# The gates of a recurrence: the weights' low part on half of the array's rows, both heads in one call

## The chip, the cores and the metric

One NeuronCore of a Trainium2 chip runs the whole layer. The metric is the device time of one execution in microseconds (us); lower is better.

## What is computed

One layer of a generator over latent tokens: 512 latent and 256 context tokens, 2048 channels, float32. The part that the change touches are the gates of the recurrence (RG-LRU): 16 heads of 64 channels, two directions, and for each a 64 by 64 matrix for the gate r and one for the gate i.

```
hl = rmsnorm(x) * (1 + sc) + sh                  # adaLN, modulation from silu(c) @ w_ada
b, c, u, g, v, q = split(hl @ w_in)              # and the same for the context
ya = b * conv(c * u) * silu(g)
xb = conv(v) + bias                              # 1024 channels, latent and context
r = sigmoid(blockdiag(xb, wa) + ba)              # per direction, 16 heads of 64
i = sigmoid(blockdiag(xb, wx) + bx)
log_a = -8 * r * softplus(-lam);  a = exp(log_a)
h = scan(a, sqrt(1 - exp(2 log_a)) * i * xb)     # forward and backward
out = rmsnorm(x + gt * (concat(ya, (h_f + h_b) * silu(q)) @ w_out))
```

## The kernel before

Products in float32 accuracy are made of float32r matmuls (one pass each): an operand is split into a high part and a low part, the rest, and high x high, high x low and low x high are added up in PSUM. `mm3` (lines 81 to 85) issues these three matmuls for the projections. `split_piece` (line 331) splits a piece of 1024 columns of weights: ScalarE copies the high part (line 73), VectorE subtracts (line 74).

The program has three stages on TensorE. First the adaLN products (`ada`, line 216; its matmuls carry line 223 in the profile) alternate with the first seven tiles of the projection: `ada` multiplies plain float32 operands on tiles of 128 rows by 32 columns of the array, four of them side by side, each writing 32 partitions of PSUM. Then the loop over the remaining pieces of the projection (line 616), one step for each piece of eight 128-row blocks; last the output projection. The order of the work is written out by hand: the tables `bg` and `mid` list for each step which functions run at its end or after its fourth block of matmuls. For each group m of 128 channels (two heads) and from a step b on: `l_prep` at b, one call of `l_gate` in the middle of each of the steps b+2 to b+5, `l_ix` at b+3 and b+5, `l_exp` at b+5, and then the scan. There are eight groups, so 32 calls.

`l_prep` (line 444) makes the operands. The weights `lwh` and `lwl` are the high and low parts of a tile of 128 partitions, in which the 64 rows of a head's matrices stand twice, on partitions 0 to 63 and again on 64 to 127; its 512 columns are two directions by two heads by 128 (64 for r, 64 for i). The moving operand `xs` is a tile for each head: for head 0 the high part of the head's 64 channels on partitions 0 to 63 and the low part on 64 to 127, for head 1 the other way round. A product over all 128 partitions thus gives the weights times high plus low.

`l_gate` (line 459) handles one direction and one head for all 768 columns (512 latent, 256 context): two matmuls with the high weights (512 and 256 columns, lines 468 and 469), two with the low weights (lines 470 and 471), all over 128 partitions, into a PSUM tile `plru` of two banks that exists once (bufs=1). Then two sigmoids of 64x768 on ScalarE (lines 474 and 475) write `lr` and `li`; the next call's first matmul has to wait until both have read `plru`. ScalarE runs in order, so the copies of `split_piece` stand behind these sigmoids.

Of the kernel before, what the change touches and what calls it, by code (L numbers as in the profile page):

```python
# [9 lines left out]
AF = mybir.ActivationFunctionType  # L10
# [6 lines left out]
T = 512  # L17
TC = 256
TA = T + TC
# [30 lines left out]
def tile_hybrid_layer(ctx, tc, xt, ct, xn, wada, wgt, bgt, wa_, wbc, wout, lruw, par, ident, fg, out):  # L50
    nc = tc.nc
# [39 lines left out]
    def pc(name, i=0, n=1):  # L91
        o, w = POFF[name]
        return pt[:, o + i:o + i + n]
# [157 lines left out]
    for j in range(4):  # L251
        nc.tensor.matmul(acc[5][:, 2 * j:2 * j + 2], ssum[:, 128 * j:128 * j + 128], cmean[:, 0:2],
                         start=True, stop=True, skip_group_check=True)
# [188 lines left out]
    lru = {}  # L442
# [13 lines left out]
            xs.append(t)  # L456
        lru.update(w=(hi, lo), xs=xs)

    def l_gate(m, d, h):
        hi, lo = lru["w"]  # L460
        x = lru["xs"][h]
        if h == 0:
            lru["r", d] = lp[0].tile([128, TA], F32, name="lr", bufs=3)
            lru["i", d] = lp[0].tile([128, TA], F32, name="li", bufs=3)
        ps = pa.tile([128, 2, 512], F32, name="plru", bufs=1)
        pf = ps.rearrange("p a b -> p (a b)")
        s = slice(128 * (2 * d + h), 128 * (2 * d + h) + 128)
        nc.tensor.matmul(pf[:, 0:T], hi[:, s], x[:, 0:T], start=True, stop=False)  # L468
        nc.tensor.matmul(pf[:, T:TA], hi[:, s], x[:, T:TA], start=True, stop=False)
        nc.tensor.matmul(pf[:, 0:T], lo[:, s], x[:, 0:T], start=False, stop=True)  # L470
        nc.tensor.matmul(pf[:, T:TA], lo[:, s], x[:, T:TA], start=False, stop=True)  # L471
        b = pc("gb", 4 * m + 2 * d + h)
        o = slice(64 * h, 64 * h + 64)
        nc.scalar.activation(lru["r", d][o], pf[0:64, :TA], AF.Sigmoid, bias=b[0:64])  # L474
        nc.scalar.activation(lru["i", d][o], pf[64:128, :TA], AF.Sigmoid, bias=b[64:128])  # L475

    def l_ix(m, d):
        nc.gpsimd.tensor_tensor(lru["i", d], lru["i", d], xb[m], op=ALU.mult)  # L478
# [71 lines left out]
    for m in range(NM):  # L550
        b = S_C0 + 7 * m
        if m:
            at(b, l_sqrt, m - 1)
        at(b, l_prep, m)
        if m:
            at(b + 1, l_scan, m - 1)
        for i in range(4):
            at(b + 2 + i, l_gate, m, i // 2, i % 2, q=mid)
        at(b + 3, l_ix, m, 0)
        at(b + 5, l_ix, m, 1)  # L560
        at(b + 5, l_exp, m)
        if m + 1 < NM:
            at(b + 5, lw_load, m + 1)
        at(b + 6, l_mul, m)
# [6 lines left out]
    for j in range(4):  # L571
        b = S_C0 + 1 + 2 * j + 4 * (j // 2)
# [43 lines left out]
    for s in range(N_BC):  # L616
        ti, half = divmod(s, 2)
        n, m = BC_TILES[ti]
# [12 lines left out]
        hi, lo = wsp.pop(s)  # L631
# [4 lines left out]
        for k in range(8):  # L636
# [4 lines left out]
            w = slice(128 * k, 128 * k + 128)  # L641
            mm3(accs[ti][0], hi[:, w], lo[:, w], hlat[kk], kk == 0, kk == KT - 1)
        if n == "v":
            for k in range(8):
                kk = 8 * half + k
                w = slice(128 * k, 128 * k + 128)
# [68 lines left out]
    for q in range(N_D):  # L715
        s = N_BC + q
        c, kp = divmod(q, 8)
# [14 lines left out]
        hi, lo = wsp.pop(s)  # L732
# [98 lines left out]
```

## Time and profile before

| | us |
|---|---|
| median of 3 runs (811.78 to 813.51) | 812.3 |
| the profiled execution | 810.92 |
| its span | 809.1 |
| TensorE matmuls busy | 786.8 (97%) |
| VectorE busy | 480.4 (59%) |
| ScalarE busy | 366.8 (45%) |
| GpSimd busy | 89.7 (11%) |

The span runs from the first to the last instruction of the program; busy time is the time in which at least one instruction of the engine ran. PE is TensorE's matmul, PEld its loading of the stationary operand, which the profile lists as an engine of its own; DVE is VectorE, ACT is ScalarE, POOL is GpSimd. Matmuls are pipelined: one lasts longer than the distance to the start of the next.

### The profile page before, as it was taken

To read this page: it belongs to the slowest core of one execution; us is meant where nothing else is said; L and a number is where in the kernel's file an instruction comes from. 1 tells how busy PE (TensorE), PEld (TensorE's weight loads), DVE (VectorE), ACT (ScalarE), POOL (GpSimd) and SP (SyncE) were. 2 spreads that over 40 slices of the span, in tenths; PEclk is the share of its full clock that TensorE was granted. 3 is DMA by queue.
4 is the path that set the end of the run, shared out by engine and by line. 5 is a ranking of instruction groups with operands and counts; after the bars stand their busy time and mean duration, and the time that the engine had idled before them with its cause. 6 is when DMAs were issued, how large, how long until landed. Compare 5 with 4: busy or idle time off the path is not lost.

```text
span 809.1 us, 13525 instructions
## 1 busy us (share of the span) xinstructions
PE 786.8 (97%) x5712; PEld 678.2 (84%) x5712; DVE 480.4 (59%) x643; ACT 366.8 (45%) x458; POOL 89.7 (11%) x64
## 2 busy tenths in 40 slices
PE   7899899999999999999999999999999999999995
PEld 2688687889999998888888888888888888888884
DVE  3644444888688677283829474666476834253665
ACT  4312224451111125768576857575858532222234
POOL 0000002500000000212020202020212002020200
PEclk9999999999999999999999999999999999999999
DMA  9999996225655664232323232323231753323205
GB/s 352 417 417 415 347 353 218 98 79 187 227 184 180 226 222 153 79 116 80 120 76 122 96 121 79 118 78 118 79 124 58 309 185 92 116 81 128 79 0 208
DMA packets 36494, 136.31 MB, mean 168 GB/s; under 512 B 4049, under 2 KB 6353, under 8 KB 31697
## 3 DMA queue, kind: packets, MB, share of 16 engines
q1 hardware_dynamic: 36434, 135.45, 47.0%
q8 instruction: 45, 0.74, 0.4%
q14 instruction: 15, 0.12, 0.0%
HBM read 131.24 MB, written 4.19 MB: 167 GB/s over the span
## 4 chain that ended last, share of the span: by engine, by line
PE 95%; DMA 1%; DVE 1%; issue 1%; ACT 1%; SPq 0%; ACTq 0%
PE bacc L83 22%; PE bacc L84 22%; PE bacc L85 21%; PE bacc L741 6%; PE bacc L742 6%; PE bacc L743 6%; PE bacc L223 4%; DMA xhi<-in_xt 1%; PE plru L470 1%; PE plru L468 1%; PE plru L85 1%; PE plru L742 1%; PE plru L741 1%; PE plru L84 1%; PE plru L83 1%; PE plru L743 1%
## 5 line engine op out<-in xcount | busy, mean ns | idle before, releaser
L84 PE MATMUL bacc<-xhi,wlo 128*128 128x512 f32 x736 | 280.5, 381 | 2.4 <-issue 1.8
L83 PE MATMUL bacc<-xhi,whi 128*128 128x512 f32 x736 | 281.0, 382 | 0.8 <-ACT xhi L202 0.4
L85 PE MATMUL bacc<-hlo,whi 128*128 128x512 f32 x736 | 279.2, 379 | 2.6 <-issue 2.5
L74 DVE TENSOR_TENSOR wlo<-raw,whi 128x1024 fp32r<-128x1024 f32 (+1 forms) x129 | 157.6, 1225 | 198.9 <-ACT whi L73 197.6
L73 ACT CAST whi<-raw 128x1024 fp32r<-128x1024 f32 (+1 forms) x129 | 132.7, 1031 | 211.6 <-PE bacc L85 116.3
L84 PEld LDWEIGHTS bacc<-xhi,wlo 128*128 128x128 f32 x736 | 139.1, 189 | 25.2 <-DVE wlo L74 5.1
L85 PEld LDWEIGHTS bacc<-hlo,whi 128*128 128x128 f32 x736 | 139.1, 189 | 22.7 <-issue 2.9
L83 PEld LDWEIGHTS bacc<-xhi,whi 128*128 128x128 f32 x736 | 139.1, 189 | 22.5 <-ACT whi L73 0.7
L741 PE MATMUL bacc<-whi,yhi 128*128 128x512 f32 x224 | 85.1, 380 | 0.5 <-DVE dg L671 0.5
L742 PE MATMUL bacc<-wlo,yhi 128*128 128x512 f32 x224 | 84.9, 379 | 0.0
L743 PE MATMUL bacc<-whi,ylo 128*128 128x512 f32 x224 | 84.9, 379 | 0.0
L478 POOL TENSOR_TENSOR li<-li,xb 128x768 f32<-128x768 f32 x16 | 30.8, 1925 | 365.3 <-ACT li L475 365.3
L474 ACT ACTIVATE lr<-plru,pt 64x768 f32<-64x768 f32 x32 | 28.7, 895 | 53.2 <-PE plru L471 53.0
L267 ACT ACTIVATE xhi<-xhi,sh 128x512 fp32r<-128x512 f32 x15 | 10.8, 723 | 85.9 <-DVE xhi L266 85.9
L741 PEld LDWEIGHTS bacc<-whi,yhi 128*128 128x128 f32 x224 | 42.3, 189 | 7.1 <-DVE dg L671 1.1
L743 PEld LDWEIGHTS bacc<-whi,ylo 128*128 128x128 f32 x224 | 42.3, 189 | 6.0
L742 PEld LDWEIGHTS bacc<-wlo,yhi 128*128 128x128 f32 x224 | 42.3, 189 | 6.0
L518 DVE SCALAR_TENSOR_TENSOR gacc<-raw,cs,gacc 128x1024 f32<-128x1024 f32 x32 | 39.6, 1278 | 0.0
L223 PEld LDWEIGHTS bacc<-rada,cs 128*32 128x32 f32 x2048 | 29.6, 110 | 6.8 <-issue 6.8
L84 PE MATMUL bacc<-xchi,wlo 128*128 128x256 f32 x128 | 35.2, 275 | 0.0
L85 PE MATMUL bacc<-hclo,whi 128*128 128x256 f32 x128 | 35.2, 275 | 0.0
L83 PE MATMUL bacc<-xchi,whi 128*128 128x256 f32 x128 | 35.2, 275 | 0.0
(168 smaller groups left out, 876.3 us busy)
## 6 DMA issues: line engine op xcount, KB each, us to landing
raw<-in_wbc SPq DMA_DIRECT2D x82, 512.0 KB, 3.5
rada<-in_wada SPq DMA_DIRECT2D x32, 1024.0 KB, 10.4
raw<-in_wgt SPq DMA_DIRECT2D x32, 512.0 KB, 4.7
raw<-in_wout SPq DMA_DIRECT2D x32, 512.0 KB, 3.5
raw<-in_wa_ SPq DMA_DIRECT2D x16, 448.0 KB, 11.2
xhi<-in_xt SPq DMA_DIRECT2D x16, 256.0 KB, 4.5
xr<-in_xn SPq DMA_DIRECT2D x4, 1024.0 KB, 7.7
xchi<-in_ct SPq DMA_DIRECT2D x16, 128.0 KB, 4.4
```

The costliest lines, as they stand in the source:

```text
L73: nc.scalar.copy(hi[:, :n], raw[:, :n])
L74: nc.vector.tensor_tensor(lo[:, :n], raw[:, :n], hi[:, :n].bitcast(F32), op=ALU.subtract)
L83: nc.tensor.matmul(acc, wh, hh, start=first, stop=False)
L84: nc.tensor.matmul(acc, wl, hh, start=False, stop=False)
L85: nc.tensor.matmul(acc, wh, hl, start=False, stop=last)
L223: nc.tensor.matmul(o[32 * q:32 * q + 32], cs[:, 8 * p + j, :], r[:, j, q, :], start=p + j == 0, stop=p + j == 8, skip_group_check=True)
L474: nc.scalar.activation(lru["r", d][o], pf[0:64, :TA], AF.Sigmoid, bias=b[0:64])
L478: nc.gpsimd.tensor_tensor(lru["i", d], lru["i", d], xb[m], op=ALU.mult)
L518: nc.vector.scalar_tensor_tensor(gacc[:, s], gtq.pop(i), cs[:, k, 0:1], gacc[:, s], op0=ALU.mult, op1=ALU.add)
L741: nc.tensor.matmul(accs[t], yh[:, ts], wh, start=kk == 0, stop=False)
L742: nc.tensor.matmul(accs[t], yh[:, ts], wl, start=False, stop=False)
L743: nc.tensor.matmul(accs[t], yl[:, ts], wh, start=False, stop=kk == KT - 1)
```

## The change

One call of `l_gate` now handles one direction, both heads and half of the columns (384). The high products come first, one for each head, over all 128 partitions, each into a bank of its own. The low products follow, one for each head, over the 64 partitions only on which that head's high part stands (0 to 63 for head 0, 64 to 127 for head 1); the product of the two low parts is left out. Four sigmoids of 64x384 follow in place of two of 64x768. In the program that is built, the low products carry a tile size of 64 rows by 128 columns, at row 0 and at row 64; all other matmuls of this stage have 128 by 128. The call sites and the steps stay as they are, so that the last argument, which was the head, is now the half.

```diff
-    def l_gate(m, d, h):
+    def l_gate(m, d, c):
...
-        x = lru["xs"][h]
-        if h == 0:
+        n = TA // 2
+        cols = slice(n * c, n * c + n)
+        if c == 0:
...
         ps = pa.tile([128, 2, 512], F32, name="plru", bufs=1)
-        pf = ps.rearrange("p a b -> p (a b)")
-        s = slice(128 * (2 * d + h), 128 * (2 * d + h) + 128)
-        nc.tensor.matmul(pf[:, 0:T], hi[:, s], x[:, 0:T], start=True, stop=False)
-        nc.tensor.matmul(pf[:, T:TA], hi[:, s], x[:, T:TA], start=True, stop=False)
-        nc.tensor.matmul(pf[:, 0:T], lo[:, s], x[:, 0:T], start=False, stop=True)
-        nc.tensor.matmul(pf[:, T:TA], lo[:, s], x[:, T:TA], start=False, stop=True)
-        b = pc("gb", 4 * m + 2 * d + h)
-        o = slice(64 * h, 64 * h + 64)
-        nc.scalar.activation(lru["r", d][o], pf[0:64, :TA], AF.Sigmoid, bias=b[0:64])
-        nc.scalar.activation(lru["i", d][o], pf[64:128, :TA], AF.Sigmoid, bias=b[64:128])
+        w = [slice(128 * (2 * d + h), 128 * (2 * d + h) + 128) for h in range(2)]
+        for h in range(2):
+            nc.tensor.matmul(ps[:, h, :n], hi[:, w[h]], lru["xs"][h][:, cols], start=True, stop=False)
+        for h in range(2):
+            o = slice(64 * h, 64 * h + 64)
+            nc.tensor.matmul(ps[:, h, :n], lo[o, w[h]], lru["xs"][h][o, cols], start=False, stop=True)
+        for h in range(2):
+            b = pc("gb", 4 * m + 2 * d + h)
+            o = slice(64 * h, 64 * h + 64)
+            nc.scalar.activation(lru["r", d][o, cols], ps[0:64, h, :n], AF.Sigmoid, bias=b[0:64])
+            nc.scalar.activation(lru["i", d][o, cols], ps[64:128, h, :n], AF.Sigmoid, bias=b[64:128])
```

TensorE around the first gate call, in the kernel before (`plru<-xs,lwh` writes the gates' PSUM tile from the split input and the high weights, `lwl` are the low weights; the sizes are those of the output):

```order
L85 MATMUL bacc<-hlo,whi 128x512
L468 MATMUL plru<-xs_3416,lwh 128x512
L469 MATMUL plru<-xs_3416,lwh 128x256
L470 MATMUL plru<-xs_3416,lwl 128x512
L471 MATMUL plru<-xs_3416,lwl 128x256
L83 MATMUL bacc<-xhi,whi 128x512
```

The same place in the changed kernel (`xs_3416` is head 0's input, `xs_3419` head 1's):

```order
L85 MATMUL bacc<-hlo,whi 128x512
L470 MATMUL plru<-xs_3416,lwh 128x384
L470 MATMUL plru<-xs_3419,lwh 128x384
L473 MATMUL plru<-xs_3416,lwl 128x384
L473 MATMUL plru<-xs_3419,lwl 128x384
L83 MATMUL bacc<-xhi,whi 128x512
```

The place among the projection's matmuls and the number of matmuls are the same; the first call now reads both heads' input. ScalarE at the first two calls, before:

```order
L474 ACTIVATE lr<-plru,pt 64x768
L475 ACTIVATE li<-plru,pt 64x768
L73 CAST whi<-raw 128x1024
L474 ACTIVATE lr<-plru,pt 64x768
L475 ACTIVATE li<-plru,pt 64x768
L538 COPY gacc<-bacc 128x512
```

and now:

```order
L477 ACTIVATE lr<-plru,pt 64x384
L478 ACTIVATE li<-plru,pt 64x384
L477 ACTIVATE lr<-plru,pt 64x384
L478 ACTIVATE li<-plru,pt 64x384
L73 CAST whi<-raw 128x1024
L477 ACTIVATE lr<-plru,pt 64x384
L478 ACTIVATE li<-plru,pt 64x384
```

Each pair of sigmoids has become two pairs of half the columns, and the copy of the weights' high part stands behind four instructions instead of two. The other engines' orders are unchanged.

## Rows read from the trace of the kernel before

**Rows 1.** The page: span, busy time of TensorE, granted clock in 40 slices.
```profile
span 809.1 us, 13525 instructions
...
PE 786.8 (97%) x5712; PEld 678.2 (84%) x5712; DVE 480.4 (59%) x643; ACT 366.8 (45%) x458; POOL 89.7 (11%) x64
...
PEclk9999999999999999999999999999999999999999
```

**Rows 2.** The page: the chain that ended last, by engine.
```profile
PE 95%; DMA 1%; DVE 1%; issue 1%; ACT 1%; SPq 0%; ACTq 0%
```

**Rows 3.** Groups of TensorE, 311 to 607 us: count, busy us, mean ns, idle before.
```profile
L85 PE MATMUL bacc<-hlo,whi 128*128 128x512 f32 x421 | 159.6, 379 | 0.0
...
L468 PE MATMUL plru<-xs,lwh 128*128 128x512 f32 x32 | 12.6, 395 | 0.0
```

**Rows 4.** Timeline of TensorE round one gate call: start us, us, instruction.
```profile
391.53 0.40 PE L468 MATMUL plru<-xs,lwh 128*128 128x512 f32 x1
391.76 0.28 PE L469 MATMUL plru<-xs,lwh 128*128 128x256 f32 x1
391.88 0.40 PE L470 MATMUL plru<-xs,lwl 128*128 128x512 f32 x1
392.12 0.28 PE L471 MATMUL plru<-xs,lwl 128*128 128x256 f32 x1
392.23 0.38 PE L83 MATMUL bacc<-xhi,whi 128*128 128x512 f32 x1
```

**Rows 5.** Timeline of TensorE round one block of adaLN products (128*32 is the tile).
```profile
63.16 0.48 PE L84 MATMUL bacc<-xhi,wlo 128*128 128x512 f32 x1
63.48 0.38 PE L85 MATMUL bacc<-hlo,whi 128*128 128x512 f32 x1
63.79 1.99 PE L223 MATMUL bacc<-rada,cs 128*32 128x64 f32 x128
65.72 0.48 PE L83 MATMUL bacc<-xhi,whi 128*128 128x512 f32 x1
66.03 0.38 PE L84 MATMUL bacc<-xhi,wlo 128*128 128x512 f32 x1
66.25 0.38 PE L85 MATMUL bacc<-hlo,whi 128*128 128x512 f32 x1
```

**Rows 6.** Timeline of the weight loads in the same stretch.
```profile
63.79 1.83 PEld L223 LDWEIGHTS bacc<-rada,cs 128*32 128x32 f32 x128 [0.33 <-issue]
65.71 0.19 PEld L83 LDWEIGHTS bacc<-xhi,whi 128*128 128x128 f32 x1
...
66.04 0.19 PEld L85 LDWEIGHTS bacc<-hlo,whi 128*128 128x128 f32 x1
```

**Rows 7.** Timeline of TensorE: float32r projection, then float32 transposes, on one tile size.
```profile
162.03 0.38 PE L85 MATMUL bacc<-hlo,whi 128*128 128x512 f32 x1
162.25 0.38 PE L309 MATMUL bacc<-idt,rq_rc 128*128 128x128 f32 x2
```

**Rows 8.** Groups of ScalarE, 311 to 607 us: count, busy us, mean ns, idle before.
```profile
L474 ACT ACTIVATE lr<-plru,pt 64x768 f32<-64x768 f32 x32 | 28.7, 895 | 53.2 <-PE plru L471 53.0
...
L408 ACT ACTIVATE sgt<-bacc 128x512 f32<-128x512 f32 x10 | 6.0, 598 | 0.2
```

**Rows 9.** Timeline of ScalarE behind the gate call of rows 4.
```profile
392.48 1.28 ACT L474 ACT_TABLE_LOAD   x1 [2.24 <-PE plru L471]
...
394.68 0.91 ACT L475 ACTIVATE li<-plru,pt 64x768 f32<-64x768 f32 x1
```

**Rows 10.** Timeline of TensorE: the next gate call's first matmul.
```profile
397.41 0.39 PE L468 MATMUL plru<-xs,lwh 128*128 128x512 f32 x1
```

**Rows 11.** Timeline of VectorE: the split input of the last group, a piece's low part.
```profile
582.97 1.94 DVE L455 TENSOR_TENSOR xs<-xb,xs 64x768 fp32r<-64x768 f32 x2
584.94 1.22 DVE L74 TENSOR_TENSOR wlo<-raw,whi 128x1024 fp32r<-128x1024 f32 x1
```

**Rows 12.** Timeline of TensorE: the last group's first gate matmul.
```profile
586.89 0.40 PE L468 MATMUL plru<-xs,lwh 128*128 128x512 f32 x1
```

## The prediction

> **What bounds the kernel now.** I read the page first, then the chain of waits, then TensorE's groups and timeline in the stage that the change touches. The page shows TensorE's matmuls busy in 97% of a span of 809.1 us, at a granted clock that reads 9 in every slice [rows 1]: nothing can be won from the clock. The chain that ended last is TensorE by 95%, so another engine's work costs time only where TensorE comes to wait for it [rows 2]. In the stage of the recurrence, 311 to 607 us, the groups of TensorE have an idle time of 0.0 before them [rows 3]: the stream of matmuls is dense there, and time is the sum of the distances from one start to the next. Durations mislead here: a matmul of 512 columns lasts 0.38 us, but the next starts after 0.216 (392.23 to 397.41 holds the 24 projection matmuls of half a step and half the next [rows 4, 10], and 5.18 / 24 = 0.216). So every price below is a distance between starts.
>
> The timeline of one gate call (there are 32 [rows 3]) gives its price before: its first matmul starts at 391.53 and the next projection matmul at 392.23, so 0.70 us [rows 4]. The steps inside are 0.23 and 0.24 us for 512 columns and 0.12 and 0.11 for 256.
>
> **The change part by part.**
>
> *Columns.* The four matmuls have 384 columns each. No row has 384 contiguous columns; 0.235 us for 512 and 0.115 for 256 [rows 4] bound it, and half way between is 0.175. If all four ran one after another the call would cost 4 x 0.175 = 0.70 us, as now. So the split of columns alone is worth nothing; the gain can only come from the last two running at once. They use 64 rows each, the first the upper half of the array (partitions 0 to 63) and the second the lower, and write different banks of PSUM. If they overlap fully, the call needs 3 x 0.175 + 0.01 (the second issued just behind the first) = 0.535 us, a gain of 0.165.
>
> That tiles of the array can run at once is seen in the adaLN stage: 128 matmuls on tiles of 128 rows by 32 columns go from 63.79 to 65.72 [rows 5], 15 ns for each 64 columns, while 256 columns on the whole array take 0.115 us [rows 4], 29 ns for 64. For tiles that share columns and split the rows there is no row in this trace; I take it that they overlap too.
>
> *The switch of tile.* All other matmuls of this stage use the array as one 128 by 128 tile. Each gate call now goes from that to 64-row tiles and back. The only rows with a change of tile size are those round the adaLN products, and they show a price on both sides:
> - In: the last whole-array matmul starts at 63.48 and would make room at 63.70 (0.216 later). The weight load of the small tile starts at 63.79 [rows 6], not during the matmul before, as the one at 66.04 does behind the matmul at 66.03: 0.09 us lost.
> - Out: the run of small tiles reads 63.79 plus 1.99 us [rows 5], that is to 65.78; less the 0.22 us that one of them lasts, the last one starts near 65.56, and its columns have passed near 65.62. The next weight load starts at 65.71 [rows 6]: again 0.09 us.
> - After it, that load is uncovered: the matmul that starts at 65.72 has its successor at 66.03, 0.31 us instead of 0.216 [rows 5], so 0.10 more. The same 0.10 stands where a load was late for another reason (its data): 63.16 to 63.48 [rows 5]. So 0.10 is the price of a load of 128 columns that nothing covers.
>
> Could it be the data type that costs, as the adaLN operands are plain float32 and the projection's are float32r? No: at 162.03 a float32r matmul is followed by float32 transposes on the same whole-array tile, and the next start comes 0.22 us later, as always [rows 7]. So it is the tile.
>
> The columns' tiles are the nearest rows to the rows' tiles, so I take their price: in 0.09, an uncovered load 0.10 (both halves' loads together, as the four small loads went together), out 0.09 and an uncovered load 0.10. Where nothing is charged the price is 0; a gain below that is excluded, since the loads of today are already hidden entirely. The call becomes 0.175 x 3 + 0.01 + 0.09 + 0.10 + 0.09 + 0.10 = 0.915 us, against 0.70: **0.215 us more, 32 times, 6.9 us more.**
>
> The Trainium skill, TensorEngine Tiling (Array Packing), Key Properties, says that changing the tiling mode (not just the tile) drains TensorE. It speaks of rows' tiles as of columns' tiles; by it the sum is the one above. The trace agrees for columns (0.09 us on each side); no run here shows it for rows.
>
> *ScalarE.* Two sigmoids of 64x768 (0.895 us each) become four of 64x384, 64 more instructions in all. One of 384 lies between half of 0.895, 0.45, and the 0.60 that a sigmoid of 512 columns takes [rows 8]; near 0.49, so a call is read out in 1.95 instead of 1.79 us: 0.16 more (bounds 0 to 0.6). The reading frees the one buffer that the next call's first matmul needs. At the tightest kind of place, with a table load ahead of the sigmoids, the second one ends at 394.68 + 0.91 = 395.59 [rows 9], and the next call starts at 397.41 [rows 10]: 1.82 us of cover. The change uses 0.215 + 0.16, at most 0.8. So this costs nothing; were the cover gone, every call would pay the excess. The splits of the weight pieces stand behind these sigmoids on ScalarE, but a piece's low part that is ready at 584.94 + 1.22 [rows 11] is for the piece two steps on, and a step with a gate call lasts 5.9 us (391.53 to 397.41 [rows 4, 10]). GpSimd's products of the input gate start later by the same 0.4 us, and nothing on TensorE waits for them in this stage [rows 3].
>
> *An earlier need.* The first call of a group now reads both heads' split input, where it read the first head's alone. The second head's is ready at 582.97 + 1.94 = 584.91 [rows 11], the first call starts at 586.89 [rows 12]: 1.98 us of cover, free.
>
> **The sum.** The profiled execution took 810.9 us, its span of 809.1 and 1.8 around it; 810.9 + 6.9 = 817.8. The runs' median, 812.3, is 1.4 above that execution, so I give 812.3 + 6.9 = **819.2 us**.
>
> **The rivals.**
>
> *N, the switch is free (faster).* The place is the weight load of the first 64-row matmul: if it is taken during the matmul before, as the loads of the whole-array tile are, and the same on the way back, the call costs 0.535 us, 0.165 less; 32 calls give 5.3 us, 807.0. It decides from the point at which both sides together cost under 0.165 us. For it: rows' tiles keep the columns' paths as they are, and the loads of one tile size are always early. Against it: every pass from one tile size to another in rows 5 and 6 costs. The Trainium skill, TensorE: Matmul & The Clock Gate, The mechanism, says that a weight load overlaps running matmuls when its row group is another; read widely, that would let the halves' loads go early, and the time would be this rival's. No run here shows it. Chance 0.15.
>
> *H, the switch costs half.* Either side alone drains, or the drain is there and the loads are hidden: 0.535 + 0.19 = 0.725 us a call, 0.8 us in all, 813.1 (812.8 with the two drains alone). Chance 0.08.
>
> *S, the halves don't run at once, and the switch costs.* Then the change doesn't do what it says. If the second load only starts when the first is through, 0.10 more: 1.015 us a call, 10.1 us, 822.4. If the second matmul follows the first entirely, 1.08 us, 12.2 us, 824.5. For it: no rows' tiles are in the trace. Against: small tiles overlap in rows 5. Chance 0.11.
>
> *Z, no switch cost and no overlap.* 0.70 us as now, 812.3. Chance 0.04.
>
> **How the numbers follow.** The forecast keeps 0.62; its own range, with each of the four charges a little lower or higher, is 816 to 821. About 0.2% (1.6 us) is what a measurement of this kernel can tell from no change, 810.7 to 813.9. Faster: N, 0.15. Same: H and Z, 0.12. Slower: the forecast and S, 0.73. The range leaves out N and Z, 0.19, and reaches from H to the end of S: 812.5 to 824.6.
>
> **What would show it.** In the timeline after, between the first of the gate's full-row matmuls and the next projection matmul: 0.92 us where I am right, 0.54 by N, 0.70 by Z, 1.0 or more by S. The second low matmul should start about 10 ns behind the first. The first low weight load should start some 0.09 us after the second full-row matmul's columns have passed, and the step from the first projection matmul behind the call to the next should read 0.31 instead of 0.216. ScalarE should show 128 sigmoids near 0.49 us, and TensorE no wait for the gates' buffer. I am wrong if weight loads of 64-row tiles start while whole-array matmuls stream.

## The result

The changed kernel takes 818.44 us (median of 4 runs, 818.26 to 819.54) against 812.04 us before (4 runs, 811.58 to 813.51): a ratio of 1.007 with a 95% interval of 1.0055 to 1.0085 (the quotient of the two medians is 1.0079). It is 6.4 us slower; 6.9 more had been forecast.

The profiled execution took 818.47 us, its span 816.7. The page of after, to be set beside [rows 1, 2]:

```profile
span 816.7 us, 13589 instructions
...
PE 793.7 (97%) x5712; PEld 674.2 (83%) x5712; DVE 481.1 (59%) x643; ACT 382.6 (47%) x522; POOL 89.3 (11%) x64
...
PEclk9999999999999999999999999999999999999999
...
PE 95%; DMA 1%; DVE 1%; issue 1%; ACT 1%; SPq 0%; ACTq 0%
```

The granted clock and the chain are what they were. ScalarE is busier by 15.8 us. TensorE's matmuls are busy for 793.7 us instead of 786.8 [rows 1], 6.9 more for the same 5712 matmuls, and their share is still 97%. Their groups show no idle time in the recurrence; those of the weight loads do (PEld below; both from 311 to 615 us):

```profile
L83 PE MATMUL bacc<-xhi,whi 128*128 128x512 f32 x422 | 162.9, 386 | 0.0
...
L473 PE MATMUL plru<-xs,lwl 64*128 64x384 f32 x64 | 14.2, 438 | 0.0
```

```profile
L83 PEld LDWEIGHTS bacc<-xhi,whi 128*128 128x128 f32 x421 | 79.5, 189 | 16.0 <-issue 5.4
...
L473 PEld LDWEIGHTS plru<-xs,lwl 64*128 64x128 f32 x64 | 6.0, 183 | 8.0 <-issue 8.0
```

and the loads of the same line 83 before (311 to 607 us):

```profile
L83 PEld LDWEIGHTS bacc<-xhi,whi 128*128 128x128 f32 x420 | 79.3, 189 | 11.9
```

So the loss is inside "busy", where it can't be told from work, and no idle time of the matmuls shows it. The idle time of the weight loads that "issue" ended, 8.0 us ahead of the 64-row loads and 5.4 ahead of the first projection load behind them, points to the place; it is not the price, since matmuls issued before still run through most of it. The distances between starts give the price. One gate call of after in the timeline of TensorE (start us, us, instruction; beside [rows 4]):

```profile
412.17 0.51 PE L470 MATMUL plru<-xs,lwh 128*128 128x384 f32 x2
412.61 0.45 PE L473 MATMUL plru<-xs,lwl 64*128 64x384 f32 x2
412.99 0.48 PE L83 MATMUL bacc<-xhi,whi 128*128 128x512 f32 x1
413.31 0.38 PE L84 MATMUL bacc<-xhi,wlo 128*128 128x512 f32 x1
```

and its weight loads (beside [rows 6]):

```profile
411.95 0.41 PEld L470 LDWEIGHTS plru<-xs,lwh 128*128 128x128 f32 x2
412.61 0.18 PEld L473 LDWEIGHTS plru<-xs,lwl 64*128 64x128 f32 x2 [0.25 <-issue]
412.99 0.19 PEld L83 LDWEIGHTS bacc<-xhi,whi 128*128 128x128 f32 x1 [0.19 <-issue]
413.10 0.19 PEld L84 LDWEIGHTS bacc<-xhi,wlo 128*128 128x128 f32 x1
```

The call lasts 412.99 - 412.17 = 0.82 us, and the step behind it 0.32 instead of 0.216, so the call costs 0.92 us with the step behind it, against 0.70. The first 64-row weight load starts at 412.61, together with its matmul: it was not taken early. Two full-row products of 0.175 end their columns at 412.52, so 0.09 us were lost. The next projection matmul starts 0.38 behind the halves (0.37 in the median of the 32 calls), which is 0.10 for the uncovered load, 0.175 for the columns and again 0.09, and its own load is uncovered too. The two halves' starts lie 3 to 4 ns apart and merge into one row of 0.45 us.

Over the whole recurrence, the first call's start to the last call's (31 calls) went from 604.54 - 311.54 = 293.00 us to 611.88 - 312.14 = 299.74, 6.74 us or 0.217 a call. The two profiled executions differ by 7.55 us (818.47 against 810.92): with the last call 6.95 of them lie in the 32 calls, and 0.60 ahead of the first one.

### The profile page after: what moved, and what is told of

It reads as the page before. It is cut to its first block, busy times and chain, and to the rows that moved or that the text cites. A ratio compares the mean times of both kernels' runs of the same rounds, so it can differ in the third digit from the quotient of the medians.

```text
span 816.7 us, 13589 instructions
## 1 busy us (share of the span) xinstructions
PE 793.7 (97%) x5712; PEld 674.2 (83%) x5712; DVE 481.1 (59%) x643; ACT 382.6 (47%) x522; POOL 89.3 (11%) x64
## 4 chain that ended last, share of the span: by engine, by line
PE 95%; DMA 1%; DVE 1%; issue 1%; ACT 1%; SPq 0%; ACTq 0%
PE bacc L83 22%; PE bacc L84 22%; PE bacc L85 21%; PE bacc L744 6%; PE bacc L746 6%; PE bacc L745 6%; PE bacc L223 4%; PE plru L473 1%; PE plru L470 1%; DMA xhi<-in_xt 1%; PE plru L85 1%; PE plru L746 1%; PE plru L744 1%; PE plru L83 1%; PE plru L84 1%
## 5 line engine op out<-in xcount | busy, mean ns | idle before, releaser
L83 PE MATMUL bacc<-xhi,whi 128*128 128x512 f32 x736 | 284.0, 386 | 1.1 <-ACT xhi L202 0.4
L477 ACT ACTIVATE lr<-plru,pt 64x384 f32<-64x384 f32 x64 | 36.8, 576 | 50.8 <-PE plru L473 46.1
L478 ACT ACTIVATE li<-plru,pt 64x384 f32<-64x384 f32 x64 | 37.0, 577 | 1.0
```

What stands on the lines that cost most here:

```text
L83: nc.tensor.matmul(acc, wh, hh, start=first, stop=False)
L477: nc.scalar.activation(lru["r", d][o, cols], ps[0:64, h, :n], AF.Sigmoid, bias=b[0:64])
L478: nc.scalar.activation(lru["i", d][o, cols], ps[64:128, h, :n], AF.Sigmoid, bias=b[64:128])
```

## The experiments

The theory: the loss is the two changes of tile size in each call (0.385 us), less what the overlapping halves give back (0.17 us). Rival A puts it down to the split of the columns or ScalarE's longer reading, rival B says that the halves don't overlap and the changes of tile are cheaper, rival C that each 64-row matmul costs, whatever stands beside it. The runs of before beside the first four kernels have a median of 812.72 us, beside the last four of 812.82.

### The columns and both heads, without the small tile

```diff
-            nc.tensor.matmul(ps[:, h, :n], lo[o, w[h]], lru["xs"][h][o, cols], start=False, stop=True)
+            nc.tensor.matmul(ps[:, h, :n], lo[:, w[h]], lru["xs"][h][:, cols], start=False, stop=True)
```

> Both heads in one call, half of the columns, four sigmoids of 384, but the low products over all 128 rows, so no change of tile. Theory (the loss of 6.4 us is the two changes of tile in each call, 0.385 us a call, less 0.17 us that the overlapping halves give back): a call costs 0.70 us as before, the time is 812 us within 1 us. Rival A (the loss comes from the split of the columns or from the longer reading by ScalarE, 4 x 0.576 us instead of 2 x 0.896): about 818 us, with waits of TensorE for the gates' buffer or calls longer than 0.70 us.

Measured: 812.99 us (10 runs), ratio to before 1.0007 (0.9997 to 1.0017). A call of it in the timeline, 606.09 to 606.79, is 0.70 us:

```profile
606.09 0.52 PE L470 MATMUL plru<-xs,lwh 128*128 128x384 f32 x2
606.45 0.51 PE L473 MATMUL plru<-xs,lwl 128*128 128x384 f32 x2
606.79 0.38 PE L83 MATMUL bacc<-xhi,whi 128*128 128x512 f32 x1
```

From the first call's start to the last one's it is 606.09 - 313.09 = 293.00 us, as in the kernel before. Rival A falls: the columns, the earlier need of the second head's input and the four sigmoids cost nothing in the recurrence.

### The 64 rows alone

```diff
-        nc.tensor.matmul(pf[:, 0:T], lo[:, s], x[:, 0:T], start=False, stop=True)
-        nc.tensor.matmul(pf[:, T:TA], lo[:, s], x[:, T:TA], start=False, stop=True)
+        o = slice(64 * h, 64 * h + 64)
+        nc.tensor.matmul(pf[:, 0:T], lo[o, s], x[o, 0:T], start=False, stop=True)
+        nc.tensor.matmul(pf[:, T:TA], lo[o, s], x[o, T:TA], start=False, stop=True)
         b = pc("gb", 4 * m + 2 * d + h)
-        o = slice(64 * h, 64 * h + 64)
```

> The call of before (one head, 768 columns, two sigmoids), only the two low products take the 64 rows with the head's high part; they have one head's rows, so they cannot overlap. Theory: 0.70 + 0.385 = 1.09 us a call, 32 x 0.385 = 12.3 us more than before, 824.3 us. Rival A (columns or reading): 812 us. Rival B (the halves in the changed kernel do not overlap, and the two changes of tile cost only some 0.21 us a call together): 818.9 us.

Measured: 826.2 us, ratio 1.0165 (1.0145 to 1.0184), 13.5 us above before, where the theory says 12.3 (the interval is 11.8 to 15.0). From the first call's start to the last one's the trace has 305.0 us, 12.0 more than before, 0.39 for each of 31 calls or 12.4 for 32. In this kernel nothing is won back, so its timeline shows the whole price:

```profile
416.96 0.40 PE L468 MATMUL plru<-xs,lwh 128*128 128x512 f32 x1
417.19 0.28 PE L469 MATMUL plru<-xs,lwh 128*128 128x256 f32 x1
417.40 0.49 PE L471 MATMUL plru<-xs,lwl 64*128 64x512 f32 x1
417.74 0.28 PE L472 MATMUL plru<-xs,lwl 64*128 64x256 f32 x1
417.94 0.48 PE L83 MATMUL bacc<-xhi,whi 128*128 128x512 f32 x1
418.26 0.38 PE L84 MATMUL bacc<-xhi,wlo 128*128 128x512 f32 x1
```

The steps are 0.21 instead of 0.12 into the small tile, 0.34 instead of 0.235 for its uncovered load, 0.20 instead of 0.11 out of it, 0.32 instead of 0.216 behind: 0.09 + 0.10 + 0.09 + 0.10. Rival B (818.9 us) falls.

### Both low products on one half of the rows

```diff
-            nc.tensor.matmul(ps[:, h, :n], lo[o, w[h]], lru["xs"][h][o, cols], start=False, stop=True)
+            nc.tensor.matmul(ps[:, h, :n], lo[0:64, w[h]], lru["xs"][h][0:64, cols], start=False, stop=True)
```

> The changed kernel, but head 1's low product reads partitions 0 to 63 like head 0's (it multiplies the low part of the input there in place of the high part), so both have the same tile and must follow each other. Theory: 0.17 us more a call, 32 x 0.17 = 5.5 us above the changed kernel, 823.9 us; the last low matmul starts some 0.17 us behind the one before, not 3 ns. Rival B (they follow each other already): 818.4 us, the same as the changed kernel.

Measured: 825.51 us, ratio 1.016 (1.0145 to 1.0175); 12.8 us above the runs of before beside it, where the changed kernel was 6.4 above its own: 6.4 us more, where 5.5 were expected. By the trace a call went from 0.82 to 0.99 us, the columns of one more product:

```profile
415.16 0.51 PE L470 MATMUL plru<-xs,lwh 128*128 128x384 f32 x2
415.60 0.62 PE L473 MATMUL plru<-xs,lwl 64*128 64x384 f32 x2
416.15 0.48 PE L83 MATMUL bacc<-xhi,whi 128*128 128x512 f32 x1
```

From the first call's start to the last one's (313.20 to 618.36) it is 305.16 us, 5.4 above the changed kernel's 299.74. So the expected 5.5 us are shown in the recurrence. In the profiled execution another 1.06 us lie ahead of the first call, whose start differs by some us from one execution to the next (311.4 to 315.1 us in the traces of this study that have it at the same step). The halves do overlap in the changed kernel.

### Sixteen passes to the small tile

The calls of the two halves of the columns become one (the edit of the table of steps; in the call, all four full-row products come ahead of the four low ones, the second half's into two of the projection's banks):

```diff
-        for i in range(4):
-            at(b + 2 + i, l_gate, m, i // 2, i % 2, q=mid)
+        for i in range(2):
+            at(b + 3 + 2 * i, l_gate, m, i, q=mid)
```

> One call for each direction with both halves of the columns: four full-row products, then the four low products on 64-row tiles; the second half's two banks come from the projection's buffers. 16 calls, so 16 passes to the small tile and back in place of 32, with the same matmuls. Theory: a call costs 4 x 0.175 + 0.09 + 0.10 + 2 x 0.175 + 0.09 + 0.10 = 1.43 us against 2 x 0.703 in the kernel before, 16 x 0.024 = 0.4 us more, 812.4 us; against the changed kernel 6 us less. Rival C (each 64-row matmul costs, not each pass): 818.4 us. Should the projection wait for a buffer, that shows as waits of TensorE for ScalarE and adds to either.

Measured: 816.89 us, ratio 1.0052 (1.0036 to 1.0068). The calls came out as the theory says (mean 1.346 us, and 0.106 behind), but the time did not: 4.2 us above before instead of 0.4. TensorE waited where it had not, three times, for the low part of weight pieces: 2.3 us of idle time, 3.3 us by the distances between starts with the uncovered loads behind them. The longest such wait in its timeline (the bracket is the idle time ahead and what ended it), and VectorE's timeline at that place:

```profile
600.68 0.48 PE L84 MATMUL bacc<-xhi,wlo 128*128 128x512 f32 x1 [1.60 <-DVE wlo L74]
```

```profile
598.80 0.69 DVE L512 TENSOR_TENSOR xb<-li 128x512 f32<-128x512 f32 x1
599.41 1.22 DVE L74 TENSOR_TENSOR wlo<-raw,whi 128x1024 fp32r<-128x1024 f32 x1
```

The subtraction stands in VectorE's order behind the scan of the group before, which had come late: in the kernel below, with earlier calls, the same scan and sum (lines 511 and 512) are through 3.2 us sooner, and nothing waits. The prediction's cover for ScalarE's work was that of the old places of the calls; here it was gone.

### The same, one step earlier

```diff
-            at(b + 3 + 2 * i, l_gate, m, i, q=mid)
+            at(b + 2 + 2 * i, l_gate, m, i, q=mid)
```

> As e4_both_halves, but the two calls of a group stand at steps b+2 and b+4 instead of b+3 and b+5. In e4 the calls measured 1.346 us and 0.106 behind them, as the theory says, yet the time was 4.2 us above before, with TensorE waiting for the low part of weight pieces. Theory: these waits come from the place, as the last reading of the gates delays the exponentials, the square roots and then the scan, behind which VectorE's subtractions stand; an earlier call takes the waits away, and 16 x (1.452 - 1.406) = 0.7 us above before remain: 813.4 us. Rival (the longer block of eight sigmoids itself delays the pieces): 816.9 us again, with the same waits.

Measured: 813.92 us (10 runs), ratio 1.0009 (0.9997 to 1.0022). The waits are gone (TensorE's list of waits is empty from 300 to 640 us), the calls are the same (1.346 us):

```profile
601.59 0.52 PE L471 MATMUL plru<-xs,lwh 128*128 128x384 f32 x2
601.94 0.51 PE L471 MATMUL bacc<-xs,lwh 128*128 128x384 f32 x2
602.38 0.45 PE L475 MATMUL plru<-xs,lwl 64*128 64x384 f32 x2
602.66 0.34 PE L475 MATMUL bacc<-xs,lwl 64*128 64x384 f32 x2
602.93 0.48 PE L83 MATMUL bacc<-xhi,whi 128*128 128x512 f32 x1
```

With the same 64-row matmuls but half of the passes the loss is down to 1.1 us in the medians, which the interval does not tell from none; rival C (818.4 us) falls. The two kernels differ in the place of the calls alone, so the excess of the kernel above was one of place.

### Eight passes, and the control

If the pass costs 0.385 us however much work stands in it, and each pair of halves wins its columns once, a whole group in one pass must win. All products of a group go to step b+2, into six banks (512 columns in a bank for each direction and head, the 256 context columns of both directions in one bank for each head); the sigmoids stay where they were:

```diff
+        at(b + 2, l_prod, m, q=mid)
         for i in range(4):
             at(b + 2 + i, l_gate, m, i // 2, i % 2, q=mid)
```

```
for h, w, cols, ps in parts:
    nc.tensor.matmul(ps, hi[:, w], lru["xs"][h][:, cols], start=True, stop=False, skip_group_check=True)
for h, w, cols, ps in parts:
    o, x = slice(64 * h, 64 * h + 64), lru["xs"][h]
    nc.tensor.matmul(ps, lo[o, w], x[o, cols], start=False, stop=True, skip_group_check=True)
```

Both this kernel and its control also move the first two of the output gate's four splits and sums two steps later; the other two stay where they were, where the expectation says two to four steps for all.

> All products of a group in one place (step b+2), into six banks: eight full-row products, then eight low products on 64-row tiles, two at a time; 8 passes to the small tile and back in place of 32. The sigmoids (512 and 256 columns) stay spread over steps b+2 to b+5, the sums of the output gate stand two to four steps later. Theory: a group costs 1.40 + 0.09 + 0.10 + 0.70 + 0.09 + 0.10 = 2.48 us against 4 x 0.703 = 2.81, 8 x 0.33 = 2.6 us less than before: 810.1 us. Rival C (each 64-row matmul costs, not each pass): 818 us. Waits for buffers or ScalarE would show as waits of TensorE and add to either.

> As e7_one_pass, but the low products over all 128 rows. Theory: no change of tile and no overlap, 2.81 us a group, the time of before within 1 us (812.7 us), so that e7's difference to this kernel, 2.6 us, is the overlap less the passes. Rival (the new order itself moves the time): this kernel differs from before by as much as e7 does.

Measured: one pass 810.74 us (12 runs), ratio 0.9967 (0.9955 to 0.9979); the control with 128 rows 813.17 us (12 runs), ratio 1.0002 (0.999 to 1.0014). So one pass is faster than before, by 2.1 us in the medians or 0.3%, and 2.4 us below the control. A group of it, and below the second pair of its low weight loads:

```profile
587.16 0.63 PE L472 MATMUL bacc<-xs,lwh 128*128 128x512 f32 x2
...
588.33 0.40 PE L472 MATMUL plru<-xs,lwh 128*128 128x256 f32 x2
588.66 0.50 PE L475 MATMUL bacc<-xs,lwl 64*128 64x512 f32 x2
589.00 0.28 PE L475 MATMUL plru<-xs,lwl 64*128 64x256 f32 x2
589.12 0.40 PE L475 MATMUL bacc<-xs,lwl 64*128 64x512 f32 x2
589.35 0.28 PE L475 MATMUL plru<-xs,lwl 64*128 64x256 f32 x2
589.56 0.48 PE L83 MATMUL bacc<-xhi,whi 128*128 128x512 f32 x1
```

```profile
588.77 0.19 PEld L475 LDWEIGHTS plru<-xs,lwl 64*128 64x128 f32 x2
```

And a group of the control, where the low products follow each other:

```profile
586.70 0.63 PE L472 MATMUL bacc<-xs,lwh 128*128 128x512 f32 x2
...
588.11 0.63 PE L475 MATMUL bacc<-xs,lwl 128*128 128x512 f32 x2
...
589.50 0.38 PE L83 MATMUL bacc<-xhi,whi 128*128 128x512 f32 x1
```

One pass takes 2.40 us (587.16 to 589.56) and 0.10 behind, against 2.80: 0.30 us less. From the first group's start to the last one's it is 273.26 us against 275.26, 0.29 for each of seven groups, so 2.3 for eight. (The two profiled executions took the same time within 0.1 us, as the first group of the one-pass kernel starts 2.5 us later, 313.91 against 311.43.) Inside the small-tile block a pair of 512 columns starts 0.34 us ahead of the next at first (its load is uncovered), later 0.23: there the loads are early again, as the pair at 588.77 is for the matmuls at 589.00. Neither kernel shows a wait of TensorE in this stage.

### A sigmoid without its bias

```diff
-            nc.scalar.activation(lru["r", d][o, cols], ps[0:64, h, :n], AF.Sigmoid, bias=b[0:64])
-            nc.scalar.activation(lru["i", d][o, cols], ps[64:128, h, :n], AF.Sigmoid, bias=b[64:128])
+            nc.scalar.activation(lru["r", d][o, cols], ps[0:64, h, :n], AF.Sigmoid)
+            nc.scalar.activation(lru["i", d][o, cols], ps[64:128, h, :n], AF.Sigmoid)
```

> The changed kernel with the gates' biases left out of the sigmoids. The prediction priced a sigmoid of 64x384 at 0.49 us by the one of 512 columns without a bias (0.598); 0.576 was measured. If the bias column is what costs, the sigmoids here take about 0.49 us; if a sigmoid that reads 64 partitions or PSUM at these columns simply has that fixed cost, 0.576 stays. The time stays that of the changed kernel within 1 us either way, as ScalarE has cover.

ScalarE's group in this kernel, and in the changed one:

```profile
L477 ACT ACTIVATE lr<-plru 64x384 f32<-64x384 f32 x64 | 31.0, 484 | 54.5 <-PE plru L473 54.1
```

```profile
L477 ACT ACTIVATE lr<-plru,pt 64x384 f32<-64x384 f32 x64 | 36.8, 576 | 50.8 <-PE plru L473 46.1 <-issue 4.2
```

0.484 us without the bias, 0.576 with it. It took 821.5 us, in a single timed run, 3 more than the changed kernel, which is outside the 1 us expected. The recurrence does not hold them: from the first call's start at 315.09 to the last one's at 614.82 it is 299.73 us, as in the changed kernel (299.74). The first call starts 2.95 us later (312.14 in the changed kernel), so they lie ahead of it, where the two programs are the same. There TensorE is busy for 3.19 us of 130 to 135, against 4.83, and twice the granted clock falls from 2.4 to 1.2 GHz for part of a stretch: it is 0.50 and 0.67 of full in 40 to 42 and 42 to 44 us and 0.66 in 135 to 140, against 1.00 in the changed kernel. The lag behind that kernel grows from 0.2 us at 39 us to 1.2 at 45, and from 1.1 at 127 to 2.95 at 140; it then stays. The runs of the kernel before beside this one spread from 811.43 to 817.06, so a single run can be off by as much, and these 3 us say nothing of the bias.

## Why the prediction was right

*What bounds.* TensorE's stream of matmuls, with no idle time; it stayed so [rows 1, 3]. The loss shows in no wait, but in longer distances between starts, as forecast.

*Columns.* 0.175 us for 384 columns was taken half way between two rows; 0.173 to 0.180 were measured, and the kernel with the columns alone costs nothing.

*The overlap of the halves.* An assumption, since no row had tiles of 64 rows; it came out, by the halves' starts and by the kernel that puts both on one half, where a call is 0.17 us longer.

*The switch of tile.* Carried over from the columns' tiles [rows 5, 6], also an assumption; 0.09, 0.10, 0.09 and 0.10 us came back, on rows' tiles, in the changed kernel and in the one with the 64 rows alone. The drain that the Trainium skill states for a change of tiling mode (TensorEngine Tiling (Array Packing), Key Properties) is therefore there for rows as for columns. Rival N, the free switch, is out: the 64-row loads start 0.09 us after the columns before have passed, not while they stream, although their rows are half of the array's. H (half of the cost) and Z are out by the same rows, S by the halves' starts. The prediction set the data type aside by rows 7, which show only the way into float32 matmuls; here the operands on both sides of the change are float32r, so the type is out without them.

*The sum.* 0.915 us a call forecast, 0.92 measured; 6.9 us forecast, 6.95 over the 32 calls in the traces, 6.4 in the medians.

*ScalarE's reading.* The mis-sized term: 0.49 us for a sigmoid of 64x384 was forecast, 0.576 measured. It was drawn from the sigmoid of 512 columns [rows 8], which has no bias column (a bias for each partition), while the gates' have one; without it 0.484 was measured. A call is read out in some 2.35 us instead of 1.95. This changed no time, since the cover holds: at a place like that of [rows 9, 10], the last sigmoid ends at 437.85 + 0.58 = 438.43 and the next call starts at 439.92, 1.49 us later.

```profile
437.85 0.58 ACT L478 ACTIVATE li<-plru,pt 64x384 f32<-64x384 f32 x1
```

```profile
439.92 0.52 PE L470 MATMUL plru<-xs,lwh 128*128 128x384 f32 x2
```

## What to carry to other kernels

Tiles of half of the rows let two products with 64 rows run in the time of one, but a stream of whole-array matmuls pays some 0.385 us for each visit to them and back, whatever the visit holds. Count the visits: with 0.175 us won by a pair of 384 columns one pair in a visit loses, two come out nearly even (1.452 us against 1.406 before), and a whole group (two pairs of 512 and two of 256 columns) wins. And price it by distances between starts: busy time grows by the loss without saying where, the matmuls' idle time shows none of it, and the weight loads' idle time shows the place alone.

## What the runs showed of the hardware that was not expected

A bias column costs ScalarE 0.09 us in each sigmoid of 64x384 (0.576 against 0.484 us). The Trainium skill, ScalarE: Activation LUTs, What ACT_TABLE_LOAD costs, gives about 93 ns for each such per-partition operand, and the runs agree. Inside a visit to the small tile the second and later pairs of loads are covered again (0.23 us between pairs of 512 columns). Only assumed before: the uncovered load of a 64-row tile costs 0.10 us as one of 128 rows does, and when both halves are loaded it is paid once.

In five of the ten traces the granted clock falls from 2.4 to 1.2 GHz near 40 us, behind a stretch in which TensorE waits; the first gate call starts at 313.2 to 315.1 us in these, and at 311.4 to 313.1 in the others that have it at the same step. What decides is not shown: from 38 to 40 us the kernel without the bias and the one with the columns alone were both busy for 0.70 us, and the clock fell in the first only.
